# Between two layers: the experts' rows summed on TensorE, GpSimd's arithmetic moved away, and the last stores put on SyncE

## The chip, the cores and the metric

The kernel runs on one core of one Trainium2 chip. The metric is the device time of one execution in microseconds; lower is better. The core has TensorE (PE, with its weight loads as PEld), VectorE (DVE), ScalarE (ACT), GpSimd (POOL) and SyncE (SP). Each takes its own instructions strictly in order, and they meet at semaphores. DMAs are issued by SP, ACT or POOL and carried by 16 shared DMA engines.

## The reference

The reference is a trunk of two layers over 1280 tokens of 1024 channels: 256 context tokens and 1024 latent ones. Each layer normalises and modulates its input to `h`, mixes tokens (an RWKV-7 scan, a windowed attention, a neighbourhood attention), adds and normalises, and then sends every token to two of 32 SwiGLU experts:

```
h = modulate(layer_norm(x));  x = layer_norm(alpha*x + mod2*mixer(h), ln1_g, ln1_b)
h = modulate(layer_norm(x));  f = w0*expert_a(h) + w1*expert_b(h)
x = layer_norm(alpha*x + mod5*f, ln2_g, ln2_b)
```

The last line of one layer, followed by the first normalisation of the next, is what happens "between the layers". The second layer no longer needs the context tokens after its mixer.

## The kernel before

**The experts.** In each layer 32 experts are run in an order worked out on the host (`expert_order`), three fixed ones first. An expert has one or more blocks of 32 to 128 tokens. `expert_block` multiplies a block by gate and up weights, applies the middle part, multiplies by the down weights, copies the result to a tile `y`, and stores `y` to a DRAM buffer `ys[l]` (L1715 and L1717); all these stores are issued by POOL. In both layers the second to last expert is one block of 64 tokens, stored as 128 rows of 2 KB, and the last one a block of 32 tokens, stored as 128 rows of 1 KB. After them stands a loop for overflow blocks (`overflow`, L1759 to L1774), whose number of turns is read on the chip. All engines pass its test (L1762), and there they wait for the DMAs that are still out. In this execution the loop makes no turn.

**Between the layers.** `layer(1)` goes over ten tiles of 128 tokens, two at a time. For each tile `combine_load` has POOL gather the tokens' two expert rows from `ys` (indirect DMAs to `cy0` and `cy1`, L1816) and load `x` to `cx`. `combine_tile` then forms `alpha*x + gate*(w0*y + w1*y1)` and its normalisation. For the first two tiles (`fast`) it works in halves of 512 columns, on ACT and DVE. For the other eight ACT scales `y` (L1841), DVE adds the second row (L1842), POOL multiplies by the gate (L1843), DVE adds `x` (L1844) and takes statistics (L1859), `norm_of` makes the mean and the reciprocal deviation with a few operations on 128x1 (L339 to L346) and a square root on ACT (L342), ACT normalises (L1869), DVE multiplies by the gain (L1872), POOL adds the bias (L1873). SP stores the result (L1956). `ln1_norm` normalises once more (L466 to L470).

`ln1_turn` turns a pair of tiles with TensorE, 2 of 8 column blocks at a time (L481, PSUM tile `pt`, two buffers), and makes two float16 parts of `h`: ACT scales and shifts to `ht` (L483), DVE rounds `ht` to `hH` (L485), POOL writes `hL = ht - hH` (L486). Then `in_A_cols` multiplies five 128-column tiles of `w_in` with that pair's columns: 24 float16 matmuls each (L528 to L530), copied out by ACT (L582). The products of one pair are written behind the next pair's tiles. The first layer uses `ln1_turn` as well.

The five weight tiles are loaded on ACT's queue between the layers (`w_tile` with `q`) and split into two float16 parts by two ACT operations (L501, L502) and one on POOL (L503); elsewhere by one on ACT and one on DVE (L505, L506).

**After the second layer** `final` runs `combine_tile` for eight tiles. There the two rows are summed on TensorE already: `w` on the diagonal of a 128x128 tile `dg` (ACT, L1850), two float32 matmuls for each half (L1855), and DVE adds `x` from PSUM (L1856). Six of these tiles still end in a POOL addition (L1873).

**Order.** The order of instructions on each engine is not the order of the text. The framework plans it from modelled durations (`schedule_with_timeline_sim=True`, L2110), and a few are marked to stay in place (`keep_in_program_order`).

Of the kernel before, what the change touches and what calls it, by code (L numbers as in the profile page):

```python
# [17 lines left out]
DEPTH = 2  # L18
D = 1024
# [3 lines left out]
P = 128  # L23
KD = D // P
# [7 lines left out]
ALPHA = (2.0 * DEPTH) ** 0.25  # L32
# [271 lines left out]
class Trunk:  # L304
# [168 lines left out]
    def ln1_turn(self, sp, ps, tag, t, xs):  # L473
        nc = self.nc
        s = 1 if t < 2 else 0
        for k0 in range(0, KD, 2):
            pt = ps.tile([P, 2, 256], F32, tag=tag, name="pt")
            ht = sp.tile([P, 2, 256], F32, tag="ht", name="ht", bufs=2)
            for k in range(2):
                for i in range(2):  # L480
                    nc.tensor.transpose(pt[:, k, i * P:i * P + P], xs[i][:, (k0 + k) * P:(k0 + k) * P + P], self.ident)  # L481
            for k in range(2):
                nc.scalar.activation(ht[:, k], pt[:, k], AF.Identity, bias=self.hb[:, k0 + k, s:s + 1], scale=self.hs[:, k0 + k, s:s + 1])  # L483
            H, Lo = (h[:, k0:k0 + 2, t * P:t * P + 256] for h in (self.hH, self.hL))
            nc.vector.tensor_copy(H, ht)  # L485
            nc.gpsimd.tensor_tensor(Lo, ht, H, OP.subtract)  # L486


    def w_tile(self, l, key, bp, sp, bufs=2, q=None):
        nc = self.nc  # L490
        o, n = COL_OFF[key]
        w = bp.tile([P, KD, P], F32, tag="w", name="w", bufs=2)
        wf = w.rearrange("p k c -> p (k c)")
        ins = (q or nc.sync).dma_start(wf[:, :KD * n], self.A["w_in"][l, :, o:o + KD * n])
        if q:
            self.tc.keep_in_program_order(ins)
        H = sp.tile([P, KD, P], F16, tag="wH", name="wH", bufs=bufs)
        Lo = sp.tile([P, KD, P], F16, tag="wL", name="wL", bufs=bufs)
        Hf, Lf = H.rearrange("p k c -> p (k c)"), Lo.rearrange("p k c -> p (k c)")
        if q:  # L500
            nc.scalar.mul(wf[:, :KD * n], wf[:, :KD * n], SC_W)  # L501
            nc.scalar.copy(Hf[:, :KD * n], wf[:, :KD * n])  # L502
            nc.gpsimd.tensor_tensor(Lf[:, :KD * n], wf[:, :KD * n], Hf[:, :KD * n], OP.subtract)  # L503
        else:
            nc.scalar.mul(Hf[:, :KD * n], wf[:, :KD * n], SC_W)  # L505
            nc.vector.scalar_tensor_tensor(Lf[:, :KD * n], wf[:, :KD * n], SC_W, Hf[:, :KD * n], OP.mult, OP.subtract)  # L506
        if n == P:
            return H, Lo, n
        return (Hf[:, :KD * n].rearrange("p (k c) -> p k c", k=KD), Lf[:, :KD * n].rearrange("p (k c) -> p k c", k=KD), n)
# [1130 lines left out]

    def expert_block(self, l, ws, hT, o, m, xp, ps, tag, ps_t, tag_t, dst, split):
        nc = self.nc
        v, a, te = nc.vector, nc.scalar, nc.tensor
        wg, wu, wd = ws
# [49 lines left out]
        def down():  # L1696
            gT = got["gT"]
            p0 = ps.tile([P, 512], F32, tag=tag, name="pd0")
            p1 = p0 if q > 1 else ps.tile([P, 512], F32, tag=tag, name="pd1")
            for k in range(4):  # L1700
                for y, (zh, zw) in enumerate(parts):
                    for i in range(max(q, 2)):
                        t = (p0, p1)[i] if q == 1 else p0[i * m:i * m + m, :n]
                        te.matmul(t, part(gT, zh)[:, k, :m], part(wd, zw)[:, k, i * n:i * n + n],  # L1704
                                  start=k == 0 and y == 0, stop=k == 3 and y == len(parts) - 1)
            y = self.yp.tile([P, D], F32, tag="y", name="y", bufs=2 if l == DEPTH - 1 else 3)
            ge = self.ge.get(q)
            s = 1.0 / SC_W if split else 1.0
            for p, c in ((p0, slice(0, n)), (p1, slice(512, 1024)))[:2 if q == 1 else 1]:
                if ge is not None:  # L1710
                    v.scalar_tensor_tensor(y[:, c], p[:, 0:n], s, ge[:, c], OP.mult, OP.mult)  # L1711
                else:
                    a.mul(y[:, c], p[:, 0:n], s)
            if q == 1:
                nc.gpsimd.dma_start(dst, y)  # L1715
            else:
                nc.gpsimd.dma_start(dst.rearrange("t (i c) -> i t c", i=q), y[:, 0:n])  # L1717

        return gates, middle, down

    def experts(self, l, wps, xp, ps, tag, ps_t, tag_t, rest):
# [34 lines left out]
        def split(r):  # L1756
            return units[r] >= SPLIT and r not in fixed

        def overflow():  # L1759
            nfix = self.fixrows(l)  # L1760
            nov = nc.values_load(self.ov_n[0:1, 0:1], min_val=0, max_val=2 * P * len(self.tiles[l]) // U)
            with self.tc.For_i(0, nov, 1) as it:  # L1762
                e = xp.tile([1, 1], I32, tag="ove", name="ove", bufs=1)
                nc.sync.dma_start(e, self.ov_e[bass.ds(it, 1)])
                reg = nc.sync.value_load(e[0:1, 0:1], min_val=0, max_val=NE - 1)
                ws = self.expert_load(l, reg, wps[0])
                ix = xp.tile([U, 1], I32, tag="ovx", name="ovx", bufs=1)
                nc.sync.dma_start(ix, self.ov_map[bass.ds(it, 1)].rearrange("b p -> p b"))
                hT = self.expert_rows(l, xp, ps_t, tag_t, ix, U, False)
                gates, middle, down = self.expert_block(l, ws, hT, 0, U, xp, ps, tag, ps_t, tag_t, self.ys[l][bass.ds(it * U + nfix, U)], False)  # L1770
                gates(0)
                gates(1)
                middle()
                down()  # L1774
# [3 lines left out]
        for j, (i, r, c) in enumerate(todo):  # L1778
            n = min(4, units[r] - 4 * c)
            for o, m in ((0, 2), (2, 1)) if n == 3 else ((0, n),):  # L1780
                row = U * (blk0[r] + 4 * c + o)
                o, m = U * o, U * m
                gates, middle, down = self.expert_block(l, loaded[r], hT, o, m, xp, ps, tag, ps_t, tag_t, self.ys[l][row:row + m], split(r))
# [43 lines left out]
    def combine_tile(self, l, fp, ps, tag, t, fast=False):  # L1827
# [7 lines left out]
        y, y1 = ys  # L1835
        w = self.wt[:, j]
        parts = [slice(512 * hf, 512 * hf + 512) for hf in range(2)]
        if l < DEPTH - 1:
            f = [y[:, c] for c in parts]
            for c in parts if fast else [slice(0, D)]:  # L1840
                a.activation(y[:, c], y[:, c], AF.Copy, scale=w[:, 0:1])  # L1841
                v.scalar_tensor_tensor(y[:, c], y1[:, c], w[:, 1:2], y[:, c], OP.mult, OP.add)  # L1842
                (v if fast else g).tensor_tensor(y[:, c], y[:, c], gate[:, c], OP.mult)  # L1843
                v.scalar_tensor_tensor(y[:, c], x[:, c], ALPHA, y[:, c], OP.mult, OP.add)  # L1844
        else:

            f, dg = [], []
            for k in range(2):
                d = fp.tile([P, P], F32, tag=f"dg{k}", name=f"dg{k}", bufs=3)
                a.activation(d, self.ident, AF.Copy, scale=w[:, k:k + 1])  # L1850
                dg.append(d)
            for c in parts:
                pf = ps.tile([P, 512], F32, tag=tag, name="pf")
                for k in range(2):
                    te.matmul(pf, dg[k], ys[k][:, c], start=k == 0, stop=k == 1)  # L1855
                v.scalar_tensor_tensor(x[:, c], x[:, c], ALPHA, pf, OP.mult, OP.add)  # L1856
                f.append(x[:, c])
# [256 lines left out]
```

## Time and profile before

| | |
|---|---|
| three runs | 3547.73, 3548.71 (median), 3562.64 us |
| the profiled execution | 3544.36 us, of which its span is 3541.6 us |
| busy, share of the span | PE 83%, PEld 52%, DVE 65%, ACT 44%, POOL 28% |
| mean granted TensorE clock | 0.894 of full speed |
| experts of the first layer end, second layer's first gather | about 1764 us, 1776.55 us |
| last parts of the second layer's `h` | about 1935 us |
| experts of the second layer end, end of the span | about 3471 us, 3541.6 us |

Durations below come from the profiled execution and are in microseconds from the span's start. In a timeline row the first number is the start, the second how long the merged instructions took together, xN how many there are, and the bracket says how long the engine sat idle before them and what ended that. In a group row (by line) the numbers are total busy time, the mean of one in ns, and idle time before them. Where a row has three numbers with slashes they are the shortest, median and longest in ns.

### The profile page before, as it was taken

To read this page: it belongs to the slowest core of one execution; us is meant where nothing else is said; L and a number is where in the kernel's file an instruction comes from. 1 tells how busy PE (TensorE), PEld (TensorE's weight loads), DVE (VectorE), ACT (ScalarE), POOL (GpSimd) and SP (SyncE) were. 2 spreads that over 40 slices of the span, in tenths; PEclk is the share of its full clock that TensorE was granted. 3 is DMA by queue.
4 is the path that set the end of the run, shared out by engine and by line. 5 is a ranking of instruction groups with operands and counts; after the bars stand their busy time and mean duration, and the time that the engine had idled before them with its cause. 6 is when DMAs were issued, how large, how long until landed. Compare 5 with 4: busy or idle time off the path is not lost. (4 is left out here: it accounts for less than half of the span.)

```text
span 3541.6 us, 71217 instructions
## 1 busy us (share of the span) xinstructions
PE 2930.6 (83%) x28620; PEld 1833.0 (52%) x28620; DVE 2285.5 (65%) x4614; ACT 1544.1 (44%) x2769; POOL 1007.7 (28%) x998
## 2 busy tenths in 40 slices
PE   7998889989998788888737998898889866778864
PEld 4656567666755444443325565666666443334431
DVE  4356877368769454557678677783776845554775
ACT  4342444345643154456544434443565314343651
POOL 1122453134424211111165225331433321101113
PEclk9998889999999899999858988899899978888987
DMA  9764343282355789999862542433732769899995
GB/s 375 297 194 111 80 104 89 70 237 71 113 176 199 278 315 384 385 379 367 334 227 78 158 106 77 105 103 95 200 107 73 258 235 363 338 393 364 349 347 198
DMA packets 425468, 773.11 MB, mean 218 GB/s; under 512 B 211152, under 2 KB 340848, under 8 KB 394160
## 3 DMA queue, kind: packets, MB, share of 16 engines
q1 hardware_dynamic: 388048, 697.84, 56.7%
q0 software_dynamic: 36368, 68.07, 5.7%
q8 instruction: 227, 3.72, 0.4%
q10 hardware_dynamic: 720, 2.62, 0.3%
q14 instruction: 105, 0.86, 0.1%
HBM read 653.31 MB, written 114.97 MB: 217 GB/s over the span
## 5 line engine op out<-in xcount | busy, mean ns | idle before, releaser
L1664 PE MATMUL pgate<-wgp,hT 128*32 128x256 f16 (+2 forms) x1704 | 353.1, 376 | 101.8 <-ACT wgp L1613 60.8
L1664 PEld LDWEIGHTS <-hT 128*32 128x32 f16 (+2 forms) x3408 | 206.7, 108 | 334.0 <-issue 172.7
L529 PE MATMUL acc<-hL,wH 128*128 128x256 f16 (+2 forms) x1040 | 346.4, 334 | 13.4 <-POOL hL L486 13.4
L528 PE MATMUL acc<-hH,wH 128*128 128x256 f16 (+2 forms) x1040 | 345.6, 335 | 7.6 <-DVE hH L485 6.6
L530 PE MATMUL acc<-hH,wL 128*128 128x256 f16 (+2 forms) x1040 | 345.4, 333 | 0.0
L1704 PE MATMUL pd<-wdp,gT 128*32 128x256 f16 (+2 forms) x1704 | 221.1, 369 | 37.6 <-DVE gT L1691 21.6
L1195 POOL TENSOR_SCALAR s<-s,rd 128x640 f32<-128x640 f32 (+2 forms) x216 | 171.6, 794 | 222.3 <-DVE rd L1191 97.4
L1622 POOL DMA_INDIRECT xg<-hmoe,map x69 | 87.7, 1271 | 508.4 <-PE ptx L1628 454.5
L1664 PE MATMUL pgate<-wup,hT 128*32 128x256 f16 (+1 forms) x1224 | 196.9, 347 | 19.8 <-DVE wup L1614 12.7
L1614 DVE SCALAR_TENSOR_TENSOR wgp<-wg,wgp 128x2048 f16<-128x2048 f32 x74 | 166.4, 2287 | 63.2 <-ACT wgp L1613 63.1
L1614 DVE SCALAR_TENSOR_TENSOR wdp<-wd,wdp 128x2048 f16<-128x2048 f32 x74 | 166.5, 2287 | 46.9 <-ACT wdp L1613 46.9
L1184 ACT ACTIVATE s<-s,nm 128x640 f32<-128x640 f32 (+2 forms) x216 | 164.4, 763 | 66.1 <-DVE nm L1181 48.6
L1614 DVE SCALAR_TENSOR_TENSOR wup<-wu,wup 128x2048 f16<-128x2048 f32 x74 | 166.3, 2286 | 30.0 <-ACT wup L1613 27.7
L1208 PE MATMUL po<-pt,vt 128*64 128x128 f32 x1920 | 166.9, 288 | 20.2 <-DVE pt L1199 11.7
L1293 PE MATMUL acco<-wo,o 128*128 128x512 f16 x756 | 177.2, 388 | 0.0
L1704 PEld LDWEIGHTS <-gT 128*32 128x32 f16 (+2 forms) x1704 | 97.0, 108 | 147.4 <-DVE gT L1691 30.0
L1613 ACT ACTIVATE wdp<-wd 128x2048 f16<-128x2048 f32 x74 | 137.2, 1903 | 51.0 <-DMA wd<-w_down 44.1
L1717 POOL DMA_DIRECT2D ys<-y x66 | 51.7, 784 | 378.5 <-DVE y L1711 206.9
L1613 ACT ACTIVATE wup<-wu 128x2048 f16<-128x2048 f32 x74 | 137.3, 1903 | 48.7 <-DMA wu<-w_up 48.7
L1613 ACT ACTIVATE wgp<-wg 128x2048 f16<-128x2048 f32 x74 | 137.4, 1902 | 46.0 <-DMA wg<-w_gate 42.7
L1165 PE MATMUL pss<-k,qs 128*128 128x256 f16 (+1 forms) x552 | 127.5, 269 | 31.9 <-DVE mx L1178 18.4
L1672 ACT ACTIVATE sg<-pgate 64x512 f32<-64x512 f32 (+2 forms) x86 | 42.8, 498 | 251.9 <-PE pgate L1664 251.9
(420 smaller groups left out, 7424.2 us busy)
## 6 DMA issues: line engine op xcount, KB each, us to landing
wu<-w_up SPq DMA_DIRECT2D x64, 2048.0 KB
wd<-w_down SPq DMA_DIRECT2D x64, 2048.0 KB
wg<-w_gate SPq DMA_DIRECT2D x64, 2048.0 KB
wmod<-w_mod SPq DMA_DIRECT2D x48, 1024.0 KB
w<-w_in SPq DMA_DIRECT2D x41, 512.0 KB
ld<-ys SPq DMA_DIRECT2D x40, 384.0 KB
z<-inv SPq DMA_DIRECT2D x80, 128.0 KB
ys<-y POOLq DMA_DIRECT2D x20, 512.0 KB
```

Source lines behind the costliest of these rows:

```text
L528: self.nc.tensor.matmul(ov, H[:, k, :], hh, start=k == 0, stop=False)
L529: self.nc.tensor.matmul(ov, H[:, k, :], hl, start=False, stop=False)
L530: self.nc.tensor.matmul(ov, Lo[:, k, :], hh, start=False, stop=k == KD - 1)
L1165: te.matmul(pss[:, o:o + n], qs[:, e, Q], k1[:, e, k0:k0 + n], start=True, stop=False)
L1184: a.activation(s2[:, e, :nk], s2[:, e, :nk], AF.Exp, bias=nm[:, e:e + 1], scale=1.0 / SS, accum_out=den[:, e:e + 1])
L1195: g.tensor_scalar(s2[:, e, :nk], s2[:, e, :nk], rd[:, e:e + 1], SC_Q, OP.mult, OP.mult)
L1208: te.matmul(po[64 * e:64 * e + 64, 0:P], vt[:, kb, 64 * e:64 * e + 64], pt[:, e, x * P:x * P + P], start=x == 0, stop=x == len(kbs) - 1)
L1293: te.matmul(acc, o[:, zo, k] if k < KD - 1 else self.og_last[:, zo, tok], wo[:, zw, k, c], start=k == 0 and y == 0, stop=k == KD - 1 and y ...
L1613: nc.scalar.mul(t[:, 0, c], w[:, c], SC_W)
L1614: nc.vector.scalar_tensor_tensor(t[:, 1, c], w[:, c], SC_W, t[:, 0, c], OP.mult, OP.subtract)
L1664: te.matmul(p[off + i * m:off + i * m + m, :n], part(hT, zh)[:, k, o:o + m], part(w, zw)[:, k, i * n:i * n + n], start=k == 0 and y == 0, ...
L1704: te.matmul(t, part(gT, zh)[:, k, :m], part(wd, zw)[:, k, i * n:i * n + n], start=k == 0 and y == 0, stop=k == 3 and y == len(parts) - 1)
```

## The change

It has four parts.

1. `combine_tile` uses the sum on TensorE between the layers too: two `dg` tiles by ACT, two float32 matmuls for each half into a PSUM tile `pf` (two buffers there), then DVE multiplies `pf` by the gate into `y`, and adds `alpha*x` into `x`. All ten tiles now end as the fast ones did, with two DVE operations for each half (L1863, L1864); ACT's normalisation L1869 and POOL's two operations are gone there.
2. `ln1_turn` (both layers): ACT makes `hH` directly from PSUM, with a second pass of the same operation, and the subtraction for `hL` goes from POOL to DVE. DVE's rounding L485 is gone.
3. `w_tile` splits the weights loaded on ACT's queue as all others: one ACT operation and one on DVE.
4. The stores of the last two experts of each layer are issued by SP instead of POOL.

```
+            H, Lo = (h[:, k0:k0 + 2, t * P:t * P + 256] for h in (self.hH, self.hL))
             for k in range(2):
-                nc.scalar.activation(ht[:, k], pt[:, k], AF.Identity, bias=..., scale=...)
-            H, Lo = (h[:, k0:k0 + 2, t * P:t * P + 256] for h in (self.hH, self.hL))
-            nc.vector.tensor_copy(H, ht)
-            nc.gpsimd.tensor_tensor(Lo, ht, H, OP.subtract)
+                for o in (ht, H):
+                    nc.scalar.activation(o[:, k], pt[:, k], AF.Identity, bias=..., scale=...)
+            nc.vector.tensor_tensor(Lo, ht, H, OP.subtract)
...
-        if q:
-            nc.scalar.mul(wf[:, :KD * n], wf[:, :KD * n], SC_W)
-            nc.scalar.copy(Hf[:, :KD * n], wf[:, :KD * n])
-            nc.gpsimd.tensor_tensor(Lf[:, :KD * n], wf[:, :KD * n], Hf[:, :KD * n], OP.subtract)
-        else:
-            nc.scalar.mul(Hf[:, :KD * n], wf[:, :KD * n], SC_W)
-            nc.vector.scalar_tensor_tensor(Lf[:, :KD * n], wf[:, :KD * n], SC_W, Hf[:, :KD * n], OP.mult, OP.subtract)
+        nc.scalar.mul(Hf[:, :KD * n], wf[:, :KD * n], SC_W)
+        nc.vector.scalar_tensor_tensor(Lf[:, :KD * n], wf[:, :KD * n], SC_W, Hf[:, :KD * n], OP.mult, OP.subtract)
...
-                nc.gpsimd.dma_start(dst, y)
+                q_st.dma_start(dst, y)
...
-                nc.gpsimd.dma_start(dst.rearrange("t (i c) -> i t c", i=q), y[:, 0:n])
+                q_st.dma_start(dst.rearrange("t (i c) -> i t c", i=q), y[:, 0:n])
...
-                gates, middle, down = self.expert_block(l, loaded[r], ..., split(r))
+                gates, middle, down = self.expert_block(l, loaded[r], ..., split(r),
+                                                        nc.sync if i >= NE - 2 else nc.gpsimd)
...
-        if l < DEPTH - 1:
-            f = [y[:, c] for c in parts]
-            for c in parts if fast else [slice(0, D)]:
-                a.activation(y[:, c], y[:, c], AF.Copy, scale=w[:, 0:1])
-                v.scalar_tensor_tensor(y[:, c], y1[:, c], w[:, 1:2], y[:, c], OP.mult, OP.add)
-                (v if fast else g).tensor_tensor(y[:, c], y[:, c], gate[:, c], OP.mult)
-                v.scalar_tensor_tensor(y[:, c], x[:, c], ALPHA, y[:, c], OP.mult, OP.add)
-        else:
...
+        f, dg = [], []
+        for k in range(2):
+            d = fp.tile([P, P], F32, tag=f"dg{k}", name=f"dg{k}", bufs=3 if l == DEPTH - 1 else 2)
+            a.activation(d, self.ident, AF.Copy, scale=w[:, k:k + 1])
+            dg.append(d)
+        for c in parts:
+            pf = ps.tile([P, 512], F32, tag=tag, name="pf")
             for k in range(2):
...
+                te.matmul(pf, dg[k], ys[k][:, c], start=k == 0, stop=k == 1)
+            if l < DEPTH - 1:
+                v.tensor_tensor(y[:, c], pf, gate[:, c], OP.mult)
+                v.scalar_tensor_tensor(x[:, c], x[:, c], ALPHA, y[:, c], OP.mult, OP.add)
+            else:
                 v.scalar_tensor_tensor(x[:, c], x[:, c], ALPHA, pf, OP.mult, OP.add)
+            f.append(x[:, c])
...
-        if fast:
+        if fast or l < DEPTH - 1:
...
-        if l < DEPTH - 1:
-            a.activation(y, y, AF.Identity, bias=nm, scale=r)
-        else:
-            a.activation(y, x, AF.Identity, bias=nm, scale=r)
+        a.activation(y, x, AF.Identity, bias=nm, scale=r)
```

## Rows read from the trace of the kernel before

**Rows 1.** Windows: start:end, length, busy PE, PEld, DVE, ACT, POOL; clock; DMA.

```profile
1783.00:1934.40 151.40, 77.56 (x542) 61.47 (x543) 134.08 (x225) 74.56 (x120) 99.20 (x58) 0.70 0.45 158
1934.40:1998.00 63.60, 63.60 (x529) 42.32 (x526) 29.87 (x31) 25.55 (x34) 2.37 (x11) 1.00 0.42 140
3491.00:3541.00 50.00, 26.79 (x60) 10.52 (x58) 45.69 (x92) 14.37 (x25) 25.43 (x18) 0.83 0.65 257
60.00:80.00 20.00, 19.55 (x160) 12.17 (x159) 14.26 (x40) 12.60 (x23) 5.83 (x4) 1.00 1.02 416
```

**Rows 2.** Timeline from the last expert of layer 0 to the first sum.

```profile
1763.43 0.38 ACT L1713 ACTIVATE y<-pd 128x256 f32<-128x256 f32 x1 [3.28 <-PEq L1762]
...
1768.26 0.70 POOL L1717 DMA_DIRECT2D ys<-y  x1 [0.35 <-issue]
...
1776.55 1.02 POOL L1816 DMA_INDIRECT cy<-ys,slot  x1 [7.12 <-DMA ys<-y]
...
1783.08 1.42 DVE L1842 SCALAR_TENSOR_TENSOR cy<-cy,wts,cy 128x512 f32<-128x512 f32 x2 [15.13 <-DMA cy<-ys,slot]
```

**Rows 3.** Waits of 1757 to 1800: waiter, releaser, total us, times, longest.

```profile
POOL zraw L569 <- DMA ys<-y: 9.7, 1, 9.7
```

**Rows 4.** Chain of waits behind layer 1's experts: start, length, what.

```profile
3474.24 8.24 DMA ys<-y
...
3482.75 4.47 DMA cy<-ys,slot
```

**Rows 5.** Timeline: the last expert's result of layer 1.

```profile
3470.36 0.42 DVE L1711 SCALAR_TENSOR_TENSOR y<-pd,ge 128x256 f32<-128x256 f32 x1 [2.06 <-PE pd L1704]
```

**Rows 6.** The chain in the scan: a store of 128 KB issued by SP.

```profile
2246.94 2.44 DMA lan<-low
```

**Rows 7.** DVE's groups by line, 1780 to 1936.

```profile
L485 DVE CAST hH<-ht 128x512 f16<-128x512 f32 x20 | 17.5, 880 | 7.7 <-ACT ht L483 7.6
L1872 DVE TENSOR_TENSOR cy<-cy,lng 128x1024 f32<-128x1024 f32 x8 | 15.6, 1956 | 1.5 <-ACT cy L1869 1.5
L345 DVE SCALAR_TENSOR_TENSOR sd<-sd 128x1 f32<-128x1 f32 x20 | 15.0, 752 | 0.2
L1842 DVE SCALAR_TENSOR_TENSOR cy<-cy,wts,cy 128x1024 f32<-128x1024 f32 x8 | 13.8, 1740 | 0.1
...
L1867 DVE SCALAR_TENSOR_TENSOR nm<-mw,sd 128x1 f32<-128x1 f32 x8 | 6.9, 861 | 0.1
L1863 DVE SCALAR_TENSOR_TENSOR cx<-cy,mw,lng 128x512 f32<-128x512 f32 x4 | 5.2, 1334 | 0.0
L1864 DVE SCALAR_TENSOR_TENSOR cx<-cx,sd,lnb 128x512 f32<-128x512 f32 x4 | 5.2, 1341 | 0.0
```

**Rows 8.** The same stretch, single lines: shortest, median and longest in ns.

```profile
L345 DVE SCALAR_TENSOR_TENSOR sd<-sd x20: 198/219/2544, 1799.0 to 1923.2; 128x1 f32<-128x1 f32 x20
...
L1867 DVE SCALAR_TENSOR_TENSOR nm<-mw,sd x8: 106/160/2781, 1817.3 to 1909.0; 128x1 f32<-128x1 f32 x8
L485 DVE CAST hH<-ht x20: 412/428/3250, 1828.1 to 1933.3; 128x512 f16<-128x512 f32 x20
L1872 DVE TENSOR_TENSOR cy<-cy,lng x8: 1212/1224/3394, 1822.0 to 1911.5; 128x1024 f32<-128x1024 f32 x8
...
L1863 DVE SCALAR_TENSOR_TENSOR cx<-cy,mw,lng x4: 737/744/3111, 1794.1 to 1806.1; 128x512 f32<-128x512 f32 x4
```

**Rows 9.** Timeline: one POOL operation and the DVE instruction beside it.

```profile
1812.88 2.64 POOL L503 TENSOR_TENSOR wL<-w,wH 128x1024 f16<-128x1024 f32 x1 [4.10 <-ACT wH L502]
...
1813.45 2.08 DVE L345 SCALAR_TENSOR_TENSOR sd<-sd 128x1 f32<-128x1 f32 x1
```

**Rows 10.** Sums on TensorE after layer 1: timeline of PE, DVE's group.

```profile
3487.35 12.06 PE L1855 MATMUL pf<-cy,dg 128*128 128x512 f32 x24 [17.05 <-DMA cy<-ys,slot]
...
L1856 DVE SCALAR_TENSOR_TENSOR cx<-cx,pf 128x512 f32<-128x512 f32 x16 | 10.7, 672 | 20.9 <-PE pf L1855 20.9
```

**Rows 11.** ACT's group of line 483, 1780 to 1936.

```profile
L483 ACT ACTIVATE ht<-pt,hb,hs 128x256 f32<-128x256 f32 x40 | 19.7, 557 | 4.5 <-POOL hL L486 3.1 <-PE pt L481 1.2
```

More of the change, by code (lines that the diff above doesn't have):

```diff
@@ L481, in ln1_turn @@
                     nc.tensor.transpose(pt[:, k, i * P:i * P + P], xs[i][:, (k0 + k) * P:(k0 + k) * P + P], self.ident)
+            H, Lo = (h[:, k0:k0 + 2, t * P:t * P + 256] for h in (self.hH, self.hL))
             for k in range(2):
-                nc.scalar.activation(ht[:, k], pt[:, k], AF.Identity, bias=self.hb[:, k0 + k, s:s + 1], scale=self.hs[:, k0 + k, s:s + 1])
-            H, Lo = (h[:, k0:k0 + 2, t * P:t * P + 256] for h in (self.hH, self.hL))
-            nc.vector.tensor_copy(H, ht)
-            nc.gpsimd.tensor_tensor(Lo, ht, H, OP.subtract)
+                for o in (ht, H):
+                    nc.scalar.activation(o[:, k], pt[:, k], AF.Identity, bias=self.hb[:, k0 + k, s:s + 1], scale=self.hs[:, k0 + k, s:s + 1])
+            nc.vector.tensor_tensor(Lo, ht, H, OP.subtract)
     def w_tile(self, l, key, bp, sp, bufs=2, q=None):
@@ L1638, in expert_rows, with expert_block @@
         return hT
-    def expert_block(self, l, ws, hT, o, m, xp, ps, tag, ps_t, tag_t, dst, split):
+    def expert_block(self, l, ws, hT, o, m, xp, ps, tag, ps_t, tag_t, dst, split, q_st):
         nc = self.nc
@@ L1769, in overflow @@
                 hT = self.expert_rows(l, xp, ps_t, tag_t, ix, U, False)
-                gates, middle, down = self.expert_block(l, ws, hT, 0, U, xp, ps, tag, ps_t, tag_t, self.ys[l][bass.ds(it * U + nfix, U)], False)
+                gates, middle, down = self.expert_block(l, ws, hT, 0, U, xp, ps, tag, ps_t, tag_t, self.ys[l][bass.ds(it * U + nfix, U)], False, nc.gpsimd)
                 gates(0)
@@ L1782, in experts @@
                 o, m = U * o, U * m
-                gates, middle, down = self.expert_block(l, loaded[r], hT, o, m, xp, ps, tag, ps_t, tag_t, self.ys[l][row:row + m], split(r))
+                gates, middle, down = self.expert_block(l, loaded[r], hT, o, m, xp, ps, tag, ps_t, tag_t, self.ys[l][row:row + m], split(r),
+                                                        nc.sync if i >= NE - 2 else nc.gpsimd)
                 gates(0)
@@ L1837, in combine_tile @@
         parts = [slice(512 * hf, 512 * hf + 512) for hf in range(2)]
-        if l < DEPTH - 1:
-            f = [y[:, c] for c in parts]
-            for c in parts if fast else [slice(0, D)]:
-                a.activation(y[:, c], y[:, c], AF.Copy, scale=w[:, 0:1])
-                v.scalar_tensor_tensor(y[:, c], y1[:, c], w[:, 1:2], y[:, c], OP.mult, OP.add)
-                (v if fast else g).tensor_tensor(y[:, c], y[:, c], gate[:, c], OP.mult)
-                v.scalar_tensor_tensor(y[:, c], x[:, c], ALPHA, y[:, c], OP.mult, OP.add)
-        else:
-            f, dg = [], []
-            for k in range(2):
[L1849 to L1855, printed above, removed]
+        f, dg = [], []
[5 more added lines that the diff above has]
+            pf = ps.tile([P, 512], F32, tag=tag, name="pf")
+            for k in range(2):
+                te.matmul(pf, dg[k], ys[k][:, c], start=k == 0, stop=k == 1)
[3 more added lines that the diff above has]
+            else:
                 v.scalar_tensor_tensor(x[:, c], x[:, c], ALPHA, pf, OP.mult, OP.add)
-                f.append(x[:, c])
+            f.append(x[:, c])
         for hf in range(2):
```

## The prediction

> **What bounds the kernel now.** I read the busy time by stretch first, to see which engine fills each part of the span that the change touches. Between the layers DVE is the one: it is busy 134.1 of the 151.4 us from the first sum to the last part of `h`, PE only 77.6, at a mean clock of 0.70; behind it PE works without a gap to 1998, at full clock [rows 1]. So `h` sets when PE's long stretch can end, and DVE sets `h`: every microsecond that the last part of `h` comes earlier should move all of the second layer. Behind the second layer's experts DVE again fills the stretch, 45.7 of 50 us up to the end of the span [rows 1].
>
> Then the timeline across the handover. The last expert's `y` is ready at 1763.81, and POOL issues its store only at 1768.26 and the first gather at 1776.55, 12.7 us behind `y`; DVE begins at 1783.08 [rows 2]. No engine computes in between. The waits say why the store is late: POOL sat 9.7 us for an earlier store to land [rows 3]. That wait is the loop's test, where each engine waits for DMAs that are out; the planner had put the last store behind it. The chain of waits shows the same pair behind the second layer, on the path that ends the kernel: 8.24 us from the store to its landing, then 4.47 for the first gather [rows 4], with `y` ready at 3470.78 [rows 5].
>
> Last, DVE's groups. In the same stretch operations on 128x1 cost a mean of 752 ns (L345) and 861 (L1867) [rows 7], although half of them take no more than 219 and 160, and the longest took 2.5 and 2.8 us [rows 8]. One was 2.08 us long, and a POOL subtraction that began before it ended at the same moment, 1815.5 [rows 9]. I read this as DVE being held while POOL's arithmetic runs.
>
> **The change, part by part.** The sum is made against the profiled execution, 3544.4 us, 2.8 more than its span and 4.3 under the median of the runs shown.
>
> *Stores on SP, layer 0.* SP has nothing else to issue there: behind the two stores stand the loop's test, one `x` load and two gate loads. A store of the last one's size, 128 KB, issued by SP landed in 2.44 us in the scan [rows 6]; as a store of POOL it took 8.24 [rows 4]. With the first, it lands at about 1766.7, and if the planner leaves it behind the loop nothing changes much, for then the loop has no late store to wait for. POOL still has to leave the loop and clear a few columns, so the first gather goes out near 1768.0: 8.5 us earlier. With the second it lands at 1772.1 and the gather comes 4.2 earlier. I take the first, since issuer and size are the same. But SP's three loads of 512 KB, which used to run while POOL waited, now run beside the first gathers. No row shows that pair; it costs between nothing and another gather's 4.5 us [rows 4]. I take 2: **-6.5**, between -4 and -8.5.
>
> For comparison, the Trainium skill's page "DMA: Bandwidth & Descriptors" (Specifications) gives the first byte about 1 us on GpSimd's path and 0.6 on SyncE's. By that the two queues are 0.4 us apart, not 5.8 as in these rows; with it this part would be near -4.6, and the same at the end. It speaks against the change's worth and is a rival below.
>
> *The same at the end.* `y` at 3470.78, landing after 2.44 and the way out of the loop give a gather at about 3474.3 in place of 3482.75 [rows 4]: -8.4; with POOL's 8.24 it is 3479.4, -3.4. Here four loads of `x` come into the way. **-6.5** again. DVE fills what follows [rows 1], so it arrives at the end of the kernel.
>
> *DVE between the layers.* Removed are the holds, mean less median times the count, from rows 7 and 8: L345 20 x 0.53 = 10.7, L485 20 x 0.45 = 9.0, L1867 8 x 0.70 = 5.6, L1872 8 x 0.73 = 5.9, L1842 (its form's median taken from L1872, of equal width) 8 x 0.52 = 4.1, L1863 and L1864 4 x 0.59 each, 4.8. Sum 40. All of POOL's arithmetic in this stretch goes; what is left on POOL are gathers and a few cleared columns.
>
> Added: each of eight tiles loses L1842, L1844, L1872 at 1.22 and L1867 at 0.16, together 3.8 [rows 8], and gets two multiplications out of PSUM and two additions, at L1856's 0.67 [rows 10], and four operations at L1863's 0.745 [rows 8], together 5.7: +1.9, x8 = 14.9. The two fast tiles lose two weighted additions of 0.745 each: -3.0. The subtraction for `hL`, priced as L1856 too, in place of the 0.43 rounding: 20 x 0.24 = +4.8. Five weight splits at 1.22: +6.1. Sum +22.8. So DVE has 134 - 40 + 23 = 117 us of work, 17 less. With the 17 us of idle time that it has now, this part is worth -17; if other engines fill what DVE leaves, 0.
>
> Those engines: ACT is busy 74.6 of the 151.4 [rows 1]. The second pass for `hH` costs what the first does, 19.7 [rows 11], and twenty `dg` tiles at most 0.56 each; without counting the passes that it loses (L1841, L1869, L501) that is 105 of some 134. PE gets ten tiles of sums. After layer 1 its records of a sum came 24 in 12.06 us, 0.50 apart, 8 for a tile (two for each matmul): 4.0 us a tile [rows 10]. If PE's clock is higher this halves. Four of ten tiles fall before the first transposes, when PE is idle anyhow. The other six put 12 to 24 us on PE's 78. PE then has 90 to 102 of 134 us and DVE 117, and they now wait for each other inside each tile, since only two `pf` buffers lie between them. I take 4 us for that: **-13**, between 0 and -17, and up to 6 more should idle time shrink because POOL's step left the chain.
>
> *The first layer's `ln1_turn`.* ACT 22 us more and POOL's step on DVE, under PE's 19.6 of 20 [rows 1]: **0**. Without that cover, a pair of column blocks would take 1.1 us of ACT (two passes of 0.56 [rows 11]) and 0.24 of DVE more, and a POOL step less.
>
> Sum: -6.5 - 13 - 6.5 = -26, so 3518.4, and **3523 us** beside the median.
>
> **The rivals.**
>
> *SP's stores land no sooner than POOL's.* Then -4.2 - 13 - 3.4 = -20.6: 3528. For it: the landing may hang on DRAM, which both write. Against: 2.44 us at equal size [rows 6]. Chance 0.12. The page of the Trainium skill named above speaks for it.
>
> *PE takes DVE's place.* The sums stand in PE's queue behind blocks of projections and DVE idles for what it saved; only the stores pay: -13, 3536. For it: PE's clock of 0.70 and its loads above. Against: DVE's 117 is still more than PE's 102. Chance 0.22.
>
> *Slower: sums stuck behind projections.* One 128-column tile of `w_in` takes 24 matmuls, and PE cannot be interrupted. If each half of the eight later tiles must wait for such a block, while the planner thinks that it does not, DVE idles with it; the stretch of PE behind `h` shows 63.6 us for 529 records [rows 1], 0.12 each, so a block is 2.9 us at full clock and twice that at half. At 5.8 for each of 16 halves it is 92 us, less 17 and 13: +62, 3611. It decides once a tile loses over 6 us: 8 x 6 = 48, which is 18 above those 30. Against it stands that the order is planned and `pf` has two buffers. Chance 0.08.
>
> The remaining 0.03 is the order of other stages: the planner works from modelled times, so a changed start can reorder the scan, by amounts that no row shows.
>
> **How the numbers follow.** My forecast has 0.55; 3509 to 3531 is its own range. Half a per cent, about what a measurement of this kernel can tell from no change, is 17.7 us: faster means under 3531, slower over 3566. Faster gets nearly all of 0.55, 0.09 of the first rival and a quarter of the second: 0.68. Slower 0.08, the same 0.24. The range goes from all bounds met and some idle time gone (-6 -8.5 - 17 - 8.4 = -40, 3509, rounded down) to the second rival with a little lost elsewhere: 3507 to 3540.
>
> **What would show it.** Right: the first gather within 5 us of the last `y` at both places; L345's mean near 0.22 between the layers; DVE busy 117 and the last part of `h` about 20 us earlier; the second layer shifted as a whole; the last 50 us as long as before. Wrong: `pf` as releaser of long DVE waits, or PE idle before a sum; a store of SP with 8 us to its landing; the stretch behind `h` longer because PE brings a backlog into it.

## The result and the profile after

The changed kernel took 3516.65 us (median), before 3548.22 beside it: ratio 0.9908, 95% interval 0.9883 to 0.9934. It is faster by about 32 us (23 to 42 by the interval), and 6 us under the forecast. Measured once more, on another chip, the ratio was 0.9936 (e5 below). The profiled execution took 3516.03, its span is 3514.4 against 3541.6.

Windows of the kernel after, columns as in [rows 1]: from DVE's first operation on a sum to the last part of `h`; the 58.8 us behind it; the last 50 us; then two stretches inside the first one.

```profile
1782.10:1920.70 138.60, 102.97 (x662) 73.93 (x661) 107.63 (x258) 74.47 (x152) 14.47 (x15) 0.86 0.49 166
1920.70:1979.50 58.80, 58.80 (x474) 37.37 (x472) 29.81 (x32) 27.04 (x35) 1.23 (x10) 1.00 0.46 153
3464.20:3514.40 50.20, 25.51 (x58) 10.41 (x57) 44.68 (x92) 13.94 (x24) 23.35 (x16) 0.80 0.62 245
...
1782.00:1822.00 40.00, 12.45 (x29) 4.86 (x27) 38.81 (x87) 14.24 (x23) 5.56 (x6) 0.70 0.78 265
...
1832.00:1892.00 60.00, 59.36 (x405) 43.82 (x404) 47.72 (x115) 31.74 (x74) 9.00 (x9) 1.00 0.42 137
```

Beside [rows 1] the reader sees three things. DVE's work fell from 134.1 to 107.6 us and the stretch from 151.4 to 138.6, so DVE has 31 us of idle time where it had 17. PE's work there rose from 77.6 to 103.0, its mean granted clock from 0.70 to 0.86. And the two halves of the stretch have different limits: DVE is full in the first 40 us, PE from 1832 to 1892, at full clock.

The timeline of the handover behind layer 0, to be held against [rows 2]:

```profile
1757.30 0.60 ACT L1708 ACTIVATE y<-pd 128x512 f32<-128x512 f32 x1 [2.90 <-PE pd L1699]
1757.92 0.70 SPq L1712 DMA_DIRECT2D ys<-y  x1
...
1766.52 0.38 ACT L1708 ACTIVATE y<-pd 128x256 f32<-128x256 f32 x1 [5.26 <-PEq L1757]
1767.14 0.34 SPq L1817 DMA_DIRECT2D cx<-xmid  x1
1767.21 0.69 POOL L564 MEMSET zraw<- 128x1 f32 x14 [19.70 <-ACTq L1757]
...
1767.55 0.60 SPq L1712 DMA_DIRECT2D ys<-y  x1
...
1772.67 1.02 POOL L1812 DMA_INDIRECT cy<-ys,slot  x1 [4.77 <-DMA ys<-y]
...
1782.19 0.69 DVE L1845 TENSOR_TENSOR cy<-pf,gate 128x512 f32<-128x512 f32 x1 [14.24 <-PE pf L1843]
```

The first gather goes out at 1772.67, 3.9 us earlier. But the loop was left at about 1767.1, as before; SP first issued a load of `x`, then the last store, and that store took until about 1772.4 to land. The last `y` was itself 3.1 us late here (1766.90 against 1763.81): 1.1 of it stems from the stages before, and for the rest PE waited 1.12 us for the last expert's weights (before 0.38, for DVE) and then ran its 32 matmuls in 3.20 us (1.93 before), at a granted clock of 0.58 from 1763.2 to 1766.5.

The chain of waits at both handovers (start, us, what), which answers to [rows 4]:

```profile
1767.55 4.86 DMA ys<-y
1772.67 5.09 DMA cy<-ys,slot
...
3439.59 7.85 DMA ys<-y
3448.89 5.17 DMA cx<-xmid
3454.19 4.88 DMA cy<-ys,slot
```

Behind layer 1 the second to last store, now SP's, still holds the path for 7.85 us.

DVE's groups between the layers, 1772.7 to 1924, columns as in [rows 7], and one line alone as in [rows 8]:

```profile
L1855 DVE SCALAR_TENSOR_TENSOR cx<-cx,mw,lng 128x512 f32<-128x512 f32 x20 | 14.1, 745 | 0.0
...
L486 DVE TENSOR_TENSOR hL<-ht,hH 128x512 f16<-128x512 f32 x20 | 13.7, 685 | 19.8 <-ACT hH L485 19.8
L1845 DVE TENSOR_TENSOR cy<-pf,gate 128x512 f32<-128x512 f32 x20 | 13.7, 683 | 19.9 <-PE pf L1843 19.8
...
L345 DVE SCALAR_TENSOR_TENSOR sd<-sd 128x1 f32<-128x1 f32 x20 | 4.2, 215 | 0.1
```

```profile
L345 DVE SCALAR_TENSOR_TENSOR sd<-sd x20: 205/216/220, 1792.2 to 1907.3; 128x1 f32<-128x1 f32 x20
```

The holds are gone: L345 has no operation above 220 ns, where the longest took 2544 [rows 8]. New are two waits: 19.8 us for `hH`, since DVE now stands in line behind ACT for `hL`, and 19.8 for `pf`, of which 14.2 are the first gather's.

Where the 27.2 us between the spans of the two profiled executions came from, stage by stage (differences of the same anchors in both traces; `zs` is a tile that DVE makes of finished projections, L598, after: L593): up to the second to last `y` of layer 0 +1.1; to the first gather -5.0 (19.8 to 14.8); to the first `zs`, just behind the last part of `h`, -11.9 (163.2 to 151.3); to the last `zs` -5.4 (109.7 to 104.3); to the second to last `y` of layer 1 -3.1; to the first gather there -4.3 (18.9 to 14.6); to the end +1.3.

### The profile page after: what moved, and what is told of

Its sections match the earlier page's. It is cut to its first block, busy times and chain, and to the rows that moved or that the text cites. A ratio compares the mean times of both kernels' runs of the same rounds, so it can differ in the third digit from the quotient of the medians.

```text
span 3514.4 us, 71454 instructions
## 1 busy us (share of the span) xinstructions
PE 2954.0 (84%) x28700; PEld 1847.8 (53%) x28700; DVE 2256.3 (64%) x4647; ACT 1561.3 (44%) x2844; POOL 888.8 (25%) x933
## 5 line engine op out<-in xcount | busy, mean ns | idle before, releaser
L1203 PEld LDWEIGHTS po<-pt,vt 128*64 128x64 f32 x1920 | 115.3, 140 | 56.4 <-DVE pt L1194 19.1
```

The source lines that it names most:

```text
L1203: te.matmul(po[64 * e:64 * e + 64, 0:P], vt[:, kb, 64 * e:64 * e + 64], pt[:, e, x * P:x * P + P], start=x == 0, stop=x == len(kbs) - 1)
```

## The experiments

My theory was that the change has two independent gains: POOL's arithmetic no longer holds DVE, and the stores sit on a faster queue. The rivals: the holds cost nothing and PE's sums bring the gain; the stores gain nothing by themselves, only through another planned order. The table has, for each kernel, the ratio to before, and three lengths from its trace: from the second to last `y` to the first gather (layer 0, layer 1), from that gather of layer 0 to the first and to the last `zs`, and DVE's busy time up to the first `zs`.

| kernel | ratio (95%) | `y` to gather | to first, last `zs` | DVE |
|---|---|---|---|---|
| before | 1 | 19.8, 18.9 | 163.2, 273.0 | 134.1 |
| after | 0.9908 (0.9883-0.9934) | 14.8, 14.6 | 151.3, 255.7 | 107.6 |
| e5 after again | 0.9936 (0.9923-0.9949) | 15.7, 18.6 | 151.0, 255.4 | 107.7 |
| e1 stores alone | 0.9962 (0.9944-0.9981) | 14.3, 13.7 | 163.4, 268.4 | 132.6 |
| e2 all but stores | 0.9945 (0.9923-0.9967) | 19.5, 20.2 | 151.7, 257.8 | 107.8 |
| e3 `hL` on POOL | 0.9927 (0.9906-0.9949) | 15.7, 18.4 | 153.9, 265.5 | 103.7 |
| e4 sums on DVE | 0.9946 (0.9930-0.9961) | 14.3, 19.3 | 161.5, 268.2 | 119.9 |
| e6 stores on ACT | 0.9921 (0.9905-0.9938) | 15.8, 20.5 | 153.2, 257.0 | 107.8 |
| e7 half on DVE | 0.9897 (0.9875-0.9919) | 14.8, 15.2 | 148.4, 254.1 | 111.3 |
| e8 POOL dummies | 0.9942 (0.9923-0.9961) | 15.3, 14.7 | 166.8, 271.1 | 129.1 |
| e9 first pair first | 0.9909 (0.9884-0.9933) | 14.6, 17.6 | 159.1, 264.3 | 109.1 |
| e10 both | 0.9899 (0.9877-0.9921) | 14.9, 14.7 | 151.1, 260.1 | 111.1 |
| e11 half again | 0.9890 (0.9869-0.9912) | 15.0, 16.6 | 148.5, 254.1 | 111.2 |

**e1: the stores alone.** On the kernel before:

```
-                nc.gpsimd.dma_start(dst, y)
+                q_st.dma_start(dst, y)
...
+                                                        nc.sync if i >= NE - 2 else nc.gpsimd)
```

> The kernel before with part 4 alone: SP issues the stores of the last two experts of each layer. From the last y of layer 0 to the first gather it was 12.7 us in before and 5.8 in the changed kernel; from the second to last y behind layer 1 to the first gather 18.9 and 14.6. Theory 1 (the stores act by themselves): both places shorten as they did in the changed kernel, by 4 to 7 and by 4, the time by 8 to 11, so 3537 to 3540 beside a median of 3548; DVE between the layers is busy 134 as before and L345 keeps its mean near 0.75. Theory 2 (SP's stores land no sooner, and what was gained there came from the planner's other order): the two places shorten by under 2 us and the time by under 3.

**e2: all but the stores.** On the kernel after:

```
-                                                        nc.sync if i >= NE - 2 else nc.gpsimd)
+                                                        nc.gpsimd)
```

> The changed kernel without part 4: POOL issues all stores. Theory 1 (the parts add): it gives back 8 to 11 us, 3525 to 3528; the first gathers come 12 to 13 us behind the last y in both layers, and the stretch from the first gather to the last part of h is as short as in the changed kernel (151 us to the first zs). Theory 2 (the stores are worth nothing by themselves): 3516 to 3519.

Both came out for theory 1, though L345's mean in e1 was 0.56 us and not 0.75. The times are 3537.8 and 3529.9 beside 3550.5, and the ratios multiply to 0.9962 x 0.9945 = 0.9907, beside 0.9908 for the whole change: the two halves add, as far as intervals of 0.002 each can tell. That it fits to the last digit is luck, since the second measurement of the whole gave 0.9936. The chain of waits behind layer 1, e1 first and then e2:

```profile
3462.19 7.84 DMA ys<-y
3470.80 4.82 DMA ys<-y
3475.89 5.32 DMA cy<-ys,slot
```

```profile
3450.99 10.06 DMA ys<-y
3462.35 8.26 DMA ys<-y
3470.88 4.23 DMA cy<-ys,slot
```

In each the first row is the second to last store, the second the last. In the four handovers where POOL issues it (before, e2), 8.3 to 8.5 us lie between the issue of the last store and the gather; in the six of after, e5 and e1 it is 5.1 to 6.0. That is 3 us, not the 5.8 that I had taken. The rest of a handover's 4 to 6 us is the second to last store: from its issue to SP's first load behind the loop it was 8.2 to 9.5 us in five of these six (12.7 in e5, below), with POOL 9.4 to 10.7. One more thing shows in e1: from the first to the last `zs` it took 105.0 us, 4.7 less than before, with the same arithmetic. The planner had put that work in another order: of DVE's 81 instructions there 16 stand in another place than before, and PE has 811 matmul records left in place of 819. After, e5 and e2 have one and the same order there.

**e3: `hL` back on POOL.**

```
-            nc.vector.tensor_tensor(Lo, ht, H, OP.subtract)
+            nc.gpsimd.tensor_tensor(Lo, ht, H, OP.subtract)
```

> The changed kernel with only the subtraction for hL back on POOL (20 of them between the layers, 1.16 us each in before; 20 more in layer 0's first stage). Theory 1 (POOL's arithmetic holds DVE): the holds come back beside it: L345's mean rises from 0.215 to 0.4 or more, DVE's long ones are up to 2 us or more, and the last part of h comes 3 to 10 us later: 3519 to 3527. Theory 2 (the holds were no loss; the change gains because PE does the sums): DVE loses 13.7 us of work, nothing else grows, and the time is 3512 to 3517.

The time, 3519.5, decides nothing: its interval overlaps that of after. The trace says more. DVE lost 13.7 us of subtractions and its busy time fell by only 3.9; L1855 alone, one line in e3's trace:

```profile
L1855 DVE SCALAR_TENSOR_TENSOR cx<-cx,mw,lng x20: 734/743/1939, 1796.9 to 1909.9; 128x512 f32<-128x512 f32 x20
```

The holds are back, though on L1855 and L346 more than on L345 (mean 244, not the 400 expected), and the last `zs` comes 10 us later after the first gather. The last part of `h`, however, came only 1.3 us later (149.3 after 148.0), not the 3 to 10 of theory 1.

**e4: the sums on ACT and DVE.** Neither `dg` nor `pf` between the layers; for each half:

```
+                a.activation(y[:, c], y[:, c], AF.Copy, scale=w[:, 0:1])
+                v.scalar_tensor_tensor(y[:, c], y1[:, c], w[:, 1:2], y[:, c], OP.mult, OP.add)
+                v.tensor_tensor(y[:, c], y[:, c], gate[:, c], OP.mult)
```

> The changed kernel with the sum of the experts' rows between the layers on ACT and DVE in place of PE: for each half ACT scales y by the first weight, DVE adds the second row with its weight (0.745 us), multiplies by the gate and adds x; no dg tiles, no pf. DVE gets 20 x 0.745 = 15 us more, PE loses 80 records, of which the last 48 stand in the stretch where PE had no gap (0.43 us each at full clock, 20.6 us). Theory 1 (DVE still sets h, as the prediction had it): 15 us later, about 3532. Theory 2 (with the holds gone PE sets h from 1832 us on): the first four tiles cost DVE 6 us more before the first projections, PE then saves 20: about 3502.

3526.8: theory 1 was nearer, DVE's 12 us more made the stretch to the last `zs` 12.5 longer. This is also the kernel without holds and without sums on PE: DVE has 14 us less work than before, yet the first `zs` comes only 1.7 earlier. A window of it shows a part of the stretch in which PE could not use what it was spared:

```profile
1868.00:1888.00 20.00, 1.56 (x15) 1.17 (x13) 19.81 (x59) 2.89 (x8) 0.00 (x0) 0.61 0.26 105
```

DVE is full, PE idles, and the mean of its granted clock is 0.61. So with all of POOL's arithmetic moved to ACT and DVE, but no sums on PE, 5 us are won up to the last `zs`; PE's sums bring the other 13. This rests on the traces. By time the sums are worth 13 us against the first measurement of the changed kernel and 4 against the second (0.9946 beside 0.9908 and 0.9936).

**e5: the changed kernel once more**, on the chip of e6 to e8.

> The changed kernel once more, on the chip of the next three. It says how much its stages vary from one profiled execution to the next: from the first gather of layer 1 to the first zs it was 151.3 us, from there to the last zs of that stage 104.3, from the last y to the first gather 5.8 and 7.3. If what the comparison rests on is sound, these come within 2 to 3 us, and the ratio to before within 0.988 to 0.993.

The stretch between the layers repeats within 0.3 us. The handover behind layer 1 does not: 18.6 after 14.6. There the chain of waits has the second to last store as

```profile
3438.08 12.34 DMA ys<-y
3451.18 5.17 DMA ys<-y
3456.63 5.32 DMA cy<-ys,slot
```

12.34 us to its landing. The same store took 7.84 in e1 and 7.85 in after. The ratio, 0.9936, is a little over the range that I gave. The DMA packets in the trace say what differs. In after the first packet of this store moved 2.2 us behind its issue and the last 5.3 us after that; in e5 it was 4.1 and 7.9 us, and up to 3446.4 the packets of POOL's store before it ran beside them (up to 3442.0 in after).

The packets also say why this store takes so long at all. Two queue rows: the second to last store in after, from 3442 to 3447, and two of the scan's 128 KB stores in before, from 2247.5 to 2249 (packets, MB, share of the 16 DMA engines):

```profile
q1 hardware_dynamic: 124, 0.25, 13.0%
```

```profile
q1 hardware_dynamic: 1055, 0.26, 66.3%
```

13% of 16 engines is the work of two. The store has 128 packets of 2 KB, 10.8 us of packet time together, and they moved two at a time while nearly nothing else did. So most of that time it does not wait for other traffic; it is itself spread thinly. The line that issues it (L1717) cuts each token's row into q pieces and makes q the outermost dimension (`i=q`), and q is 2 here and 4 for the last expert. The end of this store is marked by two packets of 4 bytes, that of the last one by four (e6), that of a store in the scan by 16. That q sets how many packets move at once fits these rows, but no run changed q, so it is not shown.

**e6: the stores on ACT.**

```
-                                                        nc.sync if i >= NE - 2 else nc.gpsimd)
+                                                        nc.scalar if i >= NE - 2 else nc.gpsimd)
```

> The changed kernel with the last two experts' stores issued by ACT in place of SP; everything else keeps its place. On SP the last store stood behind a 512 KB load of x and landed about 4.9 us after its issue, where a store of that size took 2.44 in the scan. Theory 1 (the load ahead of it on the same queue costs the rest): on ACT's queue it lands in 2.5 to 3.5 us; as ACT issues it one or two us later, behind four dg tiles, the first gathers come as in the changed kernel, and the time is the same, 3514 to 3519. Theory 2 (5 us is what a store takes beside loads, whoever issues it): gathers 1 to 2 us later at both places, 3518 to 3522. If POOL's 8 us were a matter of traffic and not of the issuer, ACT's would be 8 too and the time near 3528.

The time, 3515.4, lies in theory 1's range, but its landing does not hold. The timeline behind layer 0:

```profile
1763.98 0.58 ACTq L1712 DMA_DIRECT2D ys<-y  x1
...
1770.58 1.03 POOL L1812 DMA_INDIRECT cy<-ys,slot  x1 [5.92 <-DMA ys<-y]
```

ACT issued it the moment the loop was left, with nothing ahead of it on its own queue, and the gather went out 6.6 us later (7.3 behind layer 1). So the place behind the `x` load on SP's queue isn't what makes 5 us of 2.44. The issuer matters, by 1 to 3 us (5.4 on average on SP, 7.0 on ACT, 8.4 on POOL), but no issuer comes near the scan's 2.44 here. Two things can be read from the packets. The first one moved 2.1 to 2.4 us behind the issue on SP (after, e5, e1), 2.5 and 2.8 on ACT, 4.7 to 6.1 on POOL (before, e2). And the store's 128 packets of 1 KB then took 2.2 to 3.1 us on SP, 2 to 4 at a time, where the scan's of 256 B ran 11 at a time. The transfers that run beside it weren't taken away, so how much is theirs stays open. By time, stores on ACT and on SP can't be told apart (0.9921 and 0.9936, overlapping intervals).

**e7 and e11: the second halves of tiles 4 to 9 on ACT and DVE**, as in e4, the first halves on PE.

```
+        for hf, c in enumerate(parts):
+            if l < DEPTH - 1 and j > 3 and hf:
+                a.activation(y[:, c], y[:, c], AF.Copy, scale=w[:, 0:1])
+                v.scalar_tensor_tensor(y[:, c], y1[:, c], w[:, 1:2], y[:, c], OP.mult, OP.add)
+                v.tensor_tensor(y[:, c], y[:, c], gate[:, c], OP.mult)
+                v.scalar_tensor_tensor(x[:, c], x[:, c], ALPHA, y[:, c], OP.mult, OP.add)
+                f.append(x[:, c])
+                continue
```

> The changed kernel, but for tiles 4 to 9 between the layers the second half of 512 columns is summed on ACT and DVE, the first half on PE. PE loses 24 of the 48 sum records that stand behind the first projections (24 x 0.43 = 10.3 us at full clock), DVE gets 6 x 0.745 = 4.5 us. Theory 1 (PE sets the stretch from the first projections on, without a gap): 4 to 10 us faster, 3507 to 3513. Theory 2 (DVE still sets it, as with all sums on DVE, which cost 13 us for 20 halves): 3 to 5 us slower, 3519 to 3522.

> The kernel with the second halves of tiles 4 to 9 on ACT and DVE once more. Its time was 12.5 us under the changed kernel's on the same chip, but its stretch between the layers only 1.4 shorter. If the gain is real and lies elsewhere (the planner orders the scan and the second experts differently), the ratio to before is again near 0.990 and the stretch from the last zs to the first store of the mixer's result near 684 us (688 and 691 in the changed kernel). If it was luck: ratio near 0.993, 688.

3509.8 and 3510.1, beside 3545.8 and 3553.6: better than both kernels, and on one chip 0.4% under the changed one (0.9897 against 0.9936). But the windows of e7 and e11 up to the first `zs` say that theory 1 has little of it:

```profile
1767.40:1915.80 148.40, 103.28 (x674) 76.02 (x675) 111.31 (x265) 79.57 (x162) 21.92 (x23) 0.81 0.51 175
```

```profile
1773.30:1921.80 148.50, 102.97 (x673) 75.64 (x674) 111.18 (x264) 79.83 (x162) 21.93 (x23) 0.81 0.50 172
```

PE lost 7 us, DVE gained 4, the stretch shrank by 2.6 to 2.9 (about 1.4 up to the last `zs`). From there to the first store of the mixer's result it took 684.4 and 684.9 against 688.4 and 690.6 in the two executions of after: the planner's order of the scan is another one, and better, in a part that the edit doesn't touch. Of DVE's 1265 instructions there 223 stand in another place than in after; e5 repeats after's order in full, and e11 that of e7.

**e8: work for POOL that nobody needs.** On the kernel after, for tiles 2 to 9:

```
+                for k in range(2):
+                    dm = fp.tile([P, D], F32, tag="dm", name="dm", bufs=1)
+                    g.tensor_tensor(dm, x, self.lb2, OP.add)
```

> The changed kernel plus work for POOL that nobody needs: for each of the eight tiles 2 to 9 between the layers two additions on 128x1024 into a tile that is never read, as many and as wide as the POOL operations that the change took out of combine_tile (about 2.3 us each, 37 us in all). Nothing waits for them but POOL's own later gathers. Theory 1 (POOL's arithmetic holds DVE, and that is what DVE lost): the means of DVE's operations rise, with single ones of 2 us and more, DVE's busy time between the layers grows by 10 to 20 us, and the time by 5 to 15: 3522 to 3532. Theory 2 (no holds, or they cost nothing): DVE's means stay, 3514 to 3519.

Theory 1, by the trace: DVE's busy time is 129.1, 21.5 more with not one DVE instruction more, and the stretch 15.5 longer. The time, 3528.1, is 5.8 over that of e5, which the intervals don't separate (0.9942 and 0.9936), and it stays 18 under before on the same chip although the stretch to the first `zs` is longer than before's. What a shorter stretch is worth in time is therefore less sure than that it is shorter. DVE's groups, and one line alone:

```profile
L1855 DVE SCALAR_TENSOR_TENSOR cx<-cx,mw,lng 128x512 f32<-128x512 f32 x20 | 18.3, 953 | 0.0
...
L345 DVE SCALAR_TENSOR_TENSOR sd<-sd 128x1 f32<-128x1 f32 x20 | 9.7, 488 | 0.1
L469 DVE SCALAR_TENSOR_TENSOR nm<-mw,sd 128x1 f32<-128x1 f32 x10 | 8.1, 810 | 0.1
```

```profile
L1845 DVE TENSOR_TENSOR cy<-pf,gate x20: 669/682/693, 1791.3 to 1913.7; 128x512 f32<-128x512 f32 x20
```

and the timeline beside one of POOL's additions:

```profile
1898.70 2.68 POOL L1860 TENSOR_TENSOR dm<-cx,lnb 128x1024 f32<-128x1024 f32 x1
1899.17 1.26 DVE L466 BATCH_NORM_STATS2 st<-cx 128x6 f32<-128x512 f32 x2
1900.35 0.67 DVE L1845 TENSOR_TENSOR cy<-pf,gate 128x512 f32<-128x512 f32 x1
1900.94 0.46 DVE L345 SCALAR_TENSOR_TENSOR sd<-sd 128x1 f32<-128x1 f32 x1
```

Beside the same POOL instruction, 1898.70 to 1901.38, the statistics (one input) and the multiplication with one input in PSUM run at full speed; L345, with two inputs in SBUF, started at 1900.94 and ended at 1901.40, when POOL did. All 20 of L1845 stay under 0.7 us.

The Trainium skill's page "SBUF — State Buffer" (Who interferes with whom) says just this: a DVE instruction with two SBUF inputs and a GpSimd instruction that reads SBUF exclude each other, and whichever issues later waits until the other is through. The trace agrees: 15 DVE instructions were held, all with two SBUF inputs, and each began after POOL's. The longest L345 took 2297 ns, the shortest 206. In before a few of the held ones began up to 0.65 us ahead of POOL's recorded start, so there the order isn't shown.

**e9 and e10: the first pair first.** On the kernel after (e9) and on e7's (e10), an edge that only orders DVE's queue; `self.nms[NT + 1]` is the last small operation of tile 1's normalisation, `no_sync` stands for a dependency of order alone:

```
+                ins = v.tensor_tensor(y[:, c], pf, gate[:, c], OP.mult)
+                if j in (2, 3):
+                    self.tc.add_manual_dep(ins.ins, self.nms[NT + 1], no_sync, reason="behind the first pair")
```

> The changed kernel with one rule for the order: on DVE the first multiplication of tiles 2 and 3 between the layers stands behind the last small operation of the first pair's normalisation. In the changed kernel DVE works on the first four tiles by turns, full for 45 us, and the first hL is ready 56 us behind the first gather; DVE then waits 20 us for ACT's hH and 20 for pf. Theory 1 (that beginning on DVE sets when PE may start, and so the stretch): the first hL 15 to 20 us earlier, the stretch from the first gather to the last zs of that stage (255.5 us in two executions) shorter by 8 to 15, the time 3505 to 3514. Theory 2 (PE's work, or the later tiles on DVE, set the stretch): the first hL earlier, the stretch as long as before within 3 us, 3515 to 3522.

> The same rule, and the second halves of tiles 4 to 9 on ACT and DVE as in the run before with that edit, whose stretch from the first gather to the last zs was 254.1 us. Theory 1 (PE is the bound once it starts, and now starts earlier): both gains add, stretch 235 to 245, time 3495 to 3507. Theory 2 (with the early start DVE is the bound, and 4.5 us more on it is a loss): stretch longer than with the rule alone by 3 to 6.

Neither theory holds. The first `hL` was ready 8.5 us earlier (47.8 behind the gather in place of 56.3), and the stretch became longer, by 8.6 to 8.9 in e9 and 6.0 over e7's in e10; tiles 2 and 3 were late instead (the fifth `hL`, the first of their pair, at 82.9 in place of 65.1). Adding the half on DVE shortened it by 4.2, which speaks against DVE as the bound there. An earlier start of PE alone did not shorten the stretch; what it would do without the delay of tiles 2 and 3 this rule doesn't show. The time shows no loss either (0.9909).

## Why the prediction was right, and where it was not

**What bounds the kernel.** Right in part. Put POOL's arithmetic back on the changed kernel (e8) and the stretch is 166.8 again. But take it away without the sums on PE (e4), and DVE has 14 us less to do while the first `zs` comes only 1.7 earlier: the 12 us need both, and "every microsecond" of DVE's work does not arrive at `h`. What I did not say is that behind the change no engine would be the bound: PE is full for 60 us of the stretch, DVE for 40, and moving work either way (e4, e7) or starting earlier (e9) brings less than what is moved, or the opposite.

**The stores, -6.5 each.** By time they are worth 13 us in e1 (7 to 20 by its interval), the predicted sum, and in e2 13 against the first measurement of the changed kernel but 3 against the second. The working was wrong. The step "it lands at about 1766.7" failed twice. The planner left the last store behind the loop, and the loop was left no earlier, as the second to last store needs 8 to 9 us on SP too; and the last store landed in 4.86, not in the 2.44 of a store in the scan [rows 6]. "Issuer and size are the same" left out the third thing, how many packets move at once, 2 to 4 here and 11 there. That the agreement of the sum came all the same is luck. Behind layer 0 the handover gave 4 to 6 us, behind layer 1 between 5 and nothing (the table). Of the 13 in e1, 4.7 us behind `h` are the planner's. So the rival "SP's stores land no sooner" was half true, with -5.0 and -4.3 in the profiled execution where it had -4.2 and -3.4. The Trainium skill's page "DMA: Bandwidth & Descriptors" (Specifications) has 0.4 us between the two paths to the first byte. Where the store went out with little beside it the trace has less: its first packet moved 1.28 us behind the issue on SP (second to last store, e1) and 1.45 on POOL (before, behind layer 1). Beside the loads of `x` it was 2.1 to 2.4 and 4.7 to 6.1, so for the last store the Trainium skill's gap is too small.

**DVE between the layers, -13.** The holds were real and the unit prices right: `hL` 0.685, the multiplication out of PSUM 0.683 and the addition 0.679, for which I had 0.67; the normalisation 0.745. DVE's work fell to 107.6, not 117. About half of the difference are holds on lines that I had not counted (L1844's mean was 1524 before): instruction by instruction the holds add up to 45 us, not 40. The other half is overlap with a neighbour, which busy time counts once: 17.7 us in after (125.3 of instructions in 107.6 busy), 12.9 in before. PE's and ACT's part was sized too small. I took 4 us for DVE's waits; they grew by about 14, mostly for `hH`, because `hL` on DVE stands behind ACT's two passes, a wait that I priced only as DVE time. `h` came 11 us earlier relative to the gather, 15 in all, not 20.

**"The second layer shifted as a whole"** was wrong in the good direction. PE entered the stretch behind `h` with less left to do (444 records in the 55.5 us behind the first `zs`, without a gap, against 479 in 58.2 before), having run at a mean granted clock of 0.86 instead of 0.70, and the last `zs` came another 5.4 earlier. How much of this is PE and how much the planner's order is not settled: e1 shows 4.7 of it with no change in the arithmetic. All but the stores was worth 19.5 us by time (e2, 12 to 27 by its interval), where I had 13: by the traces this term was sized too small, 15 to 17 us up to the last `zs` (e2, after), while the time alone doesn't exclude 13.

**PE takes DVE's place, and sums stuck behind projections.** Neither came as priced, though PE was full from 1832 to 1892. DVE's waits for `pf` behind the first are under 6 us, and PE's sums were a gain of 13 up to the last `zs` (e4).

**`ln1_turn` in layer 0, 0.** From the first to the last `zs` of layer 0 it took 144.0 before, 145.4 and 144.7 after: at most 1.5 lost, and e1, which has the old `ln1_turn`, took 145.7.

**The end.** 50.2 us from DVE's first sum to the end, 50.0 before: as predicted.

## What to carry to other kernels

Work that GpSimd did "for free" beside VectorE was charged here to VectorE's instructions with two SBUF inputs, and to the cast L485, which has one (880 ns on average, half of them at most 428 [rows 7, 8]), so price it by VectorE's longest short operations, not by GpSimd's idle time. Once the engine that is full loses its lead, price the next waits as well: what was moved onto its queue waits there for its producer, and everything behind it waits too. And where a planner orders the queues, an edit also moves stages that it does not touch, by 4 to 6 us here, so compare stage lengths between anchors beside the total. A store's price needs its shape beside its size: look at how many packets moved at once.

## What was not expected of the hardware

A 128 KB store took 2.44 us to land in the scan [rows 6], but 5.1 to 6.0 on SP, 6.6 and 7.3 on ACT and 8.3 to 8.5 on POOL between the experts and the gathers, from its issue to the gather that waits for it. SP's 256 KB store behind layer 1 needed 7.85 us in one execution of the changed kernel and 12.34 in another; its packets moved two at a time, at 13% of the DMA engines, where the scan's stores reached 66%. And a DVE instruction held by POOL ended at a fixed distance behind POOL's end, however long it had been held (e8): 0.01 to 0.02 us for 128x1, 0.55 for 128x512. So an L345 that takes 0.21 us took 0.46 or 2.30.
